# Keys and queries of the attention also stored in residue order, in blocks of 512 columns

## The chip, the cores and the metric

The kernel runs on one core of one Trainium2 chip. The metric is the device time of one execution in microseconds (us). Three runs before the change took 2612.30, 2614.26 and 2615.44 us; their median is 2614.26 us.

## What is computed

One step of a layer with two mixers, for a prompt of 2048 positions and 8 sample rows. The change touches mixer A, attention with 6 heads of 64, in three dilated branches:

```python
DILATED_BRANCHES = ((128, 1), (512, 4), (2048, 16))
def dilated_prompt(q, k, v, rel_bias, window, dil):
    nk = window // dil; blk = nk; unit = blk * dil
    ...
    qb = to_blocks(q)                 # (B, nb, blk, dil, H, E)
    kc = with_prev(to_blocks(k))
    vc = with_prev(to_blocks(v))
    ...
    s = jnp.einsum('bnqrhe,bnkrhe->bnrhqk', qb, kc) * scale + bias
    s = jnp.where(mask[None, :, None, None], s, NEG)
    lse = jax.nn.logsumexp(s, axis=-1)
    p = jnp.exp(s - lse[..., None])
    o = jnp.einsum('bnrhqk,bnkrhe->bnqrhe', p, vc)
out_a = rmsnorm(combine_branches([dilated_prompt(q, k, v, rel_bias, w, d) for (w, d) in DILATED_BRANCHES]))
```

A query at position t of a branch with dilation d meets the 128 keys before it at t-d, t-2d, ... and its own. In each branch 128 queries of one residue mod d therefore meet 128 keys of the same residue and, where there are any, the 128 before them. Mixer B (an mLSTM), the output projection and an MLP follow; the change leaves them alone.

## The kernel before

The program is written for a layer that orders each engine's instructions at build time; engines then run their lists in order. Stages, in the order of the program:

- `norm_and_v`: normalises the prompt, turns it into `XT` (two halves of the columns, each as a high and a low fp32r part) and projects v.
- `project_qk` (L913): for k, then q, and for each of three groups `j` of 128 rows of weights (two heads each), six column blocks `BLK` of 340 or 344 positions. A block is 24 matmuls (8 slices by 3 products, `mm3`, L162) into a PSUM tile `pmm` (4 buffers). ScalarE (ACT) copies the result to `qhi` (rounded to fp32r), VectorE (DVE) forms the rest `qlo`, and SyncE (SP) issues the stores of both to DRAM, `q_d` and `k_d`, at L966. For k, ACT first copies to `qb`, and `to_rows` turns `qb` with TensorE (PE) transposes into rows for the output of the key cache (`kt`, L928 to L932). The bias tables (`setup_bias`) and the gates of mixer B (`setup_gates`) are set up between the k groups.
- `xbob`: the projections of mixer B, in two halves. Attention of the 8 sample rows (`sample_attn`) runs beside the first half, the prompt's attention (`attention`, L1043) beside the second half.
- The rest of `attention` is interleaved with `mlstm` by a ratio of 0.72 steps of attention to one of mLSTM.
- Output projection and MLP, to the end.

In `attention`, `load_head` (L1046) fetches, once per head, the bias tile `nb`, the queries `Q2` (64 partitions of the high part, 64 of the low part) and the keys `KH` and `KL` (the high part twice, the low part twice), each [128, 2048] fp32. Per head come the branches b = 2 (dilation 16), 1 (dilation 4) and 0 (dilation 1); per branch four groups `g` of four tiles of 128 queries. `front` (L1062) makes the scores of two tiles: per tile two matmuls, with the tile's queries as weights and 256 columns of `KH`, then of `KL`, as the moving operand. At dilation d both operands are read with a step of d elements (L1070 to L1077). DVE adds the bias and takes the minimum (L1079), ACT takes the exponential (L1081), `turn` transposes on PE, and `weigh` multiplies by the rows of v in `V` (one DMA per group, L1128; 4 buffers). Results go out as `R4` (L1108). All loads and stores of this stage are issued by SP, in one order.

## Time and profile before

| | us |
|---|---|
| median of three runs | 2614.26 |
| the profiled execution | 2603.53 |
| its span, first to last instruction | 2601.8 |
| k projection, about 107 to 192 | 85 |
| q projection, about 192 to 262 | 70 |
| mixer B projections, first half, sample attention | 262 to 400 |
| attention of the prompt | 399.5 to 1000 |
| of it beside the second half of `xbob` | 400 to 532 |
| output projection and MLP | from about 1000 |

The matmul entries of a trace overlap: an entry's duration runs from its start to its modelled end, and the next starts before that. What a matmul takes from the engine is the distance between the starts of successive rows. In the lines of groups the columns are busy time, then the mean of one in ns, then the engine's idle time just before and what ended it.

### The profile page before, as it was taken

The page shows a single profiled execution, that of the slowest core. Times are in us where ns is not written, and L with a number is a line of the kernel's source. Part 1 is how long each engine was busy: PE and PEld are TensorE (multiplying, and loading weights), DVE is VectorE, ACT ScalarE, POOL GpSimd, SP SyncE. Part 2 cuts the span into 40 slices and gives each one's busy share as a digit, 9 for nine tenths or more (in the row PEclk, how much of TensorE's full clock was granted, in tenths as well). Part 3 has the DMA queues.
Part 4 walks back from the last instruction along what each step waited for, and adds up shares of the span by engine and source line. Part 5 has one row for each costly group of instructions (what it writes and reads, how often), then busy time and mean ns, then how long its engine had stood idle before and what let it go on. Part 6 is the DMA issues. An engine that isn't in the chain of part 4 may idle for free. (4 is left out here: it accounts for less than half of the span.)

```text
span 2601.8 us, 41795 instructions
## 1 busy us (share of the span) xinstructions
PE 2494.7 (96%) x15646; PEld 2252.6 (87%) x15646; DVE 1762.8 (68%) x3163; ACT 1157.7 (44%) x2205; POOL 861.8 (33%) x435
## 2 busy tenths in 40 slices
PE   8999999999999998899999999999999999999996
PEld 7989999997888886688788778887799999999996
DVE  6333755663876658665577996778967777676875
ACT  5431223333445544333466335653345643456333
POOL 1000000002432323211435785447753333543331
PEclk9999999997999999999999999999999999999998
DMA  7674656735768645875766768758687542765332
GB/s 199 156 195 149 177 152 169 185 100 147 189 171 190 170 132 147 261 232 155 244 224 227 274 231 285 238 203 291 212 268 244 189 129 94 244 217 165 109 118 75
DMA packets 470831, 491.64 MB, mean 189 GB/s; under 512 B 116376, under 2 KB 387124, under 8 KB 466917
## 3 DMA queue, kind: packets, MB, share of 16 engines
q1 hardware_dynamic: 468804, 485.36, 61.8%
q0 software_dynamic: 1536, 3.10, 0.5%
q8 instruction: 123, 2.02, 0.3%
q14 instruction: 80, 0.65, 0.1%
q10 hardware_dynamic: 288, 0.53, 0.1%
HBM read 380.49 MB, written 124.56 MB: 194 GB/s over the span
## 5 line engine op out<-in xcount | busy, mean ns | idle before, releaser
L74 DVE TENSOR_TENSOR al<-ax,ah 128x1024 fp32r<-128x1024 f32 x222 | 396.0, 1787 | 156.8 <-ACT ah L74 156.2
L74 POOL TENSOR_TENSOR ax<-ax,ay 128x1024 f32<-128x1024 f32 x117 | 313.2, 2677 | 310.8 <-DMA ay<-in_w_ff_dram 277.3
L1577 PE MATMUL pf<-bl,ah 128*128 128x258 f32 (+1 forms) x1344 | 360.7, 323 | 10.2 <-DVE bl L74 10.2
L1543 PE MATMUL pf<-bh,ah 128*128 128x258 f32 (+1 forms) x1344 | 359.8, 322 | 10.6 <-DVE R L74 9.5
L1543 PE MATMUL pf<-bh,al 128*128 128x258 f32 (+1 forms) x1344 | 357.6, 321 | 1.6 <-DVE al L74 1.6
L1577 PE MATMUL pf<-bh,al 128*128 128x258 f32 (+1 forms) x1344 | 358.6, 321 | 0.0
L1543 PE MATMUL pf<-bl,ah 128*128 128x258 f32 (+1 forms) x1344 | 358.1, 321 | 0.0
L1577 PE MATMUL pf<-bh,ah 128*128 128x258 f32 (+1 forms) x1344 | 351.6, 322 | 6.0 <-ACT bh L74 2.9
L74 ACT ACTIVATE ah<-ax 128x1024 fp32r<-128x1024 f32 x222 | 233.8, 1054 | 216.6 <-PE pf L1577 108.5
L74 POOL TENSOR_TENSOR bx<-R,R 128x1024 f32<-128x1024 f32 (+1 forms) x80 | 245.8, 3080 | 253.7 <-DVE bl L74 253.7
L74 DVE TENSOR_TENSOR bl<-bx,bh 128x1024 fp32r<-128x1024 f32 (+1 forms) x131 | 272.7, 2086 | 35.8 <-ACT bh L74 35.2
L1577 PEld LDWEIGHTS pf<-bl,ah 128*128 128x128 f32 x1344 | 225.1, 190 | 32.9 <-DVE bl L74 13.9
L1543 PEld LDWEIGHTS pf<-bh,ah 128*128 128x128 f32 x1344 | 224.2, 190 | 31.8 <-issue 8.7
L163 PE MATMUL pmm<-x,wh 128*128 128x344 f32 (+1 forms) x768 | 249.1, 324 | 0.0
L1577 PEld LDWEIGHTS pf<-bh,ah 128*128 128x128 f32 x1344 | 223.7, 190 | 29.2 <-DVE acc L74 4.3
L165 PE MATMUL pmm<-x,wl 128*128 128x344 f32 (+1 forms) x768 | 246.6, 321 | 0.0
L164 PE MATMUL pmm<-x,wh 128*128 128x344 f32 (+1 forms) x768 | 246.1, 321 | 0.0
L1543 PEld LDWEIGHTS pf<-bh,al 128*128 128x128 f32 x1344 | 224.0, 190 | 21.6 <-DVE al L74 1.8
L1543 PEld LDWEIGHTS pf<-bl,ah 128*128 128x128 f32 x1344 | 224.7, 190 | 19.5
L1577 PEld LDWEIGHTS pf<-bh,al 128*128 128x128 f32 x1344 | 224.3, 190 | 18.9
L74 ACT ACTIVATE R<-R 128x512 f32<-128x512 f32 (+1 forms) x256 | 161.1, 630 | 126.7 <-DVE R L74 122.6
L74 DVE TENSOR_TENSOR R<-R,pf 128x512 f32<-128x512 f32 (+1 forms) x256 | 165.2, 682 | 57.0 <-PE pf L1543 35.6
(471 smaller groups left out, 4813.7 us busy)
## 6 DMA issues: line engine op xcount, KB each, us to landing
ax<-in_w_ff_dram SPq DMA_DIRECT2D x184, 512.0 KB
ay<-in_w_ff_dram SPq DMA_DIRECT2D x120, 512.0 KB
sum_d<-ax SPq DMA_DIRECT2D x40, 512.0 KB
ax<-sum_d SPq DMA_DIRECT2D x40, 512.0 KB
xt<-in_x_prompt_dram SPq DMA_DIRECT2D x31, 512.0 KB
bx<-h_d SPq DMA_DIRECT2D x26, 516.0 KB
bx<-h_d SPq DMA_DIRECT2D x26, 512.0 KB
by<-h_d SPq DMA_DIRECT2D x22, 516.0 KB
```

The source lines that it names most:

```text
L74: return tc.keep_in_program_order(f(*a, **k))
L163: pe.matmul(out, lh, rh, start=first, stop=False)
L164: pe.matmul(out, lh, rl, start=False, stop=False)
L165: pe.matmul(out, ll, rh, start=False, stop=last)
L1543: pe.matmul(pf[:, n, :w], x_, y_[:, n * w:n * w + w], start=fst, stop=lst)
L1577: pe.matmul(pf[:, n, :w], x_[:, i, dsl], y_[:, n * w:n * w + w], start=a, stop=b)
```

## The change

1. DRAM holds k twice (`k_d[0]` in natural order, `k_d[1]` in blocks of 512 with 16 residues of 32 positions each) and q three times (natural; in blocks of 512 with 4 residues of 128; all 2048 as 16 residues of 128).
2. The projections of k and q run in blocks of 512 columns, the last as 256 and 264. After `qhi` and `qlo`, one ACT copy and one DVE copy put each block in residue order (`qhd`, `qld`), and for q a second pair of copies fills `q16`. The stores grow from two arrays for each of k and q to four for k and six for q. `kt` has one buffer instead of two, and its rows go out in one DMA per block.
3. `load_head` is split. `load_q` fetches the queries of one branch, `load_k` the keys in one of the two orders. They are issued at g == 1 of the branch before (`Q2`, `KH`, `KL` still have two buffers each). Per head that is three loads of queries and two of `KH` and `KL`, in place of one each.
4. `front` reads queries contiguously in all branches, and keys in runs of 32 elements in branches 1 and 2. In branch 1 the keys of a block then stand in another order, so `load_bias_of` permutes the bias with one ACT copy per head, and `load_v` fetches the rows of v with four DMAs per group.

```diff
-    q_d = [dram.tile([DA, S], F32, name=f"q{x}_d") for x in "hl"]
-    k_d = [dram.tile([DA, S], F32, name=f"k{x}_d") for x in "hl"]
+    q_d, k_d = ([[dram.tile([DA, S], F32, name=f"{y}{x}{v}_d") for x in "hl"] for v in range(n)]
+                for y, n in (("q", 3), ("k", 2)))
...
-    def proj(psp, tag, wh, wl, bi):
-        b0, n = BLK[bi]
-        b0 -= 1024 * (bi // 3)
-        xh, xl = XT[bi // 3]
+    def proj(psp, tag, wh, wl, b0, n):
+        xh, xl = XT[b0 // 1024]
+        b0 %= 1024
...
+        by = lambda t, d: t.rearrange("p (z r) -> p r z", r=d)
+        on = lambda t, d: t.rearrange("p (r z) -> p r z", r=d)
+        q16 = []
...
+                pt = pst.tile([P, 4, P], F32, name="ptp", tag="t")
+                for i in range(4):
+                    pe.transpose(pt[:, i], qb[:, i * P:i * P + P], ident)
+                kt = ev.tile([P, 4, P], F32, name="kt", bufs=1)
+                act.activation(kt, pt, AF.Copy)
                 ko = O["p_k"][0, 0].rearrange("t h e -> t (h e)")[:, j * P:(j + 1) * P]
-                nc.sync.dma_start(ko[b0:b0 + 2 * P].rearrange("(i p) c -> p i c", p=P), kt[:, :2])
-                nc.sync.dma_start(ko[b0 + 2 * P:b0 + m], kt[:w, 2])
-            if last:
+                nc.sync.dma_start(ko[512 * g:512 * g + 512].rearrange("(i p) c -> p i c", p=P), kt)
...
+                for g in (range(4) if which == "k" else (3, 0, 1, 2)):
+                    b0 = 512 * g
+                    hi = ev.tile([P, 512], F32R, name="qhi")
+                    lo = ev.tile([P, 512], F32R, name="qlo")
+                    qb = None
+                    if which == "k" or g == 3:
+                        qb = ev.tile([P, 520], F32, name="qb", bufs=3)
+                    for c0, n in ((0, 512),) if g < 3 else ((0, 256), (256, 264)):
+                        ps = proj(psm, "mm", wh, wl, b0 + c0, n)
+                        if later:
+                            to_rows(*later.pop())
+                        m = min(n, 512 - c0)
+                        cs = slice(c0, c0 + m)
+                        if which == "k":
+                            act.activation(qb[:, c0:c0 + n], ps[:, :n], AF.Copy)
+                            split(hi[:, cs], lo[:, cs], qb[:, cs])
+                        else:
+                            act.activation(hi[:, cs], ps[:, :m], AF.Copy, scale=-0.125)
+                            vec.scalar_tensor_tensor(lo[:, cs], ps[:, :m], -0.125, hi[:, cs].bitcast(F32),
+                                                     op0=OP.mult, op1=OP.subtract)
+                            if n > m:
+                                act.activation(qb[:, 512:], ps[:, m:n], AF.Copy, scale=-0.125)
+                    d = 16 if which == "k" else 4
+                    hd_ = ev.tile([P, 512], F32R, name="qhd")
+                    ld_ = ev.tile([P, 512], F32R, name="qld")
+                    act.activation(on(hd_, d), by(hi, d).bitcast(F32), AF.Copy)
+                    vec.tensor_copy(on(ld_, d), by(lo, d).bitcast(F32))
+                    for v, two in enumerate(((hi, lo), (hd_, ld_))):
+                        for dd, tt in zip(dst[v], two):
+                            nc.sync.dma_start(dd[j * P:(j + 1) * P, b0:b0 + 512], tt.bitcast(F32))
+                    if which == "q":
+                        if g == 3:
+                            q16 = [ev16.tile([P, 16, P], F32R, name=f"q16{x}") for x in "hl"]
+                        act.activation(q16[0][:, :, 32 * g:32 * g + 32], by(hi, 16).bitcast(F32), AF.Copy)
+                        vec.tensor_copy(q16[1][:, :, 32 * g:32 * g + 32], by(lo, 16).bitcast(F32))
+                        if g == 2:
+                            for dd, tt in zip(dst[2], q16):
+                                nc.sync.dma_start(dd[j * P:(j + 1) * P], tt.rearrange("p r z -> p (r z)").bitcast(F32))
+                    if qb is not None:
+                        later.append((which, j, g, qb))
...
+                    ev16 = pool(sset, "ev16", 1, "right")
+        sset.close()
...
+        def load_bias_of(h):
+            nb = wk.tile([P, 640], F32, name="nb")
+            raw = wk.tile([P, 256], F32, name="nbr", bufs=1)
+            load_bias(raw, 1, h)
+            for b in (2, 0):
+                o, w = NBW[b]
+                load_bias(nb[:, o:o + w], b, h)
+            act.activation(nb[:, 256:512].rearrange("p (k r z) -> p k r z", k=2, r=4),
+                           raw.rearrange("p (k z r) -> p k r z", k=2, r=4), AF.Copy)
+            return nb
+
+        def load_pairs(h, *sets):
             hs = slice(HD * h, HD * h + HD)
-            nb = wk.tile([P, 640], F32, name="nb")
-            for b, (o, w) in enumerate(NBW):
-                load_bias(nb[:, o:o + w], b, h)
-            Q, KH, KL = (wk.tile([P, S], F32, name=x) for x in ("Q2", "KH", "KL"))
-            for dst, lo, hi in ((Q, q_d[0], q_d[1]), (KH, k_d[0], k_d[0]), (KL, k_d[1], k_d[1])):
+            for dst, lo, hi in sets:
                 nc.sync.dma_start(dst[:HD], lo[hs])
                 nc.sync.dma_start(dst[HD:], hi[hs])
-            return nb, Q.bitcast(F32R), KH.bitcast(F32R), KL.bitcast(F32R)
+            return [t.bitcast(F32R) for t, _, _ in sets]
+
+        def load_q(h, b):
+            return load_pairs(h, (wk.tile([P, S], F32, name="Q2"), *q_d[b]))[0]
+
+        def load_k(h, v):
+            return load_pairs(h, *((wk.tile([P, S], F32, name=n), x, x) for n, x in zip(("KH", "KL"), k_d[v])))
...
+        def load_v(V, b, g, h):
+            if b == 1:
+                rs = HD + 1
+                for r in range(4):
+                    nc.sync.dma_start(V[32 * r:32 * r + 32],
+                                      bass.AP(tensor=v_d.tensor, offset=v_d.offset + (h * S + 512 * g + 4 * r) * rs,
+                                              ap=[[16 * rs, 32], [rs, 4], [1, rs]]))
+            else:
+                nc.sync.dma_start(V, rows(v_d, b, g, HD + 1, h * S * (HD + 1), HD + 1))
...
+            g4 = lambda t: t.rearrange("p (g r z) -> p g r z", r=16, z=32)
+            g44 = lambda t: t.rearrange("p (g k r z) -> p g k r z", k=4, r=4, z=32)
             ex = wk.tile([P, 2, 256], F32, name="ex", bufs=3)
             s_ = ps.tile([P, 2, 256], F32, name="ps_s", tag="s", bufs=2)
             for e, (a, w, mn, vts) in enumerate(tiles):
                 for i, K in enumerate((KH, KL)):
-                    if w == 256:
-                        mv, out, c0 = K[:, a - P * d:a + (P - 1) * d + 1:d], s_[:, e], 0
-                    elif b == 0:
-                        mv, out, c0 = K[:, 0:256], s_[:, e], 0
+                    out, c0 = s_[:, e], 0
+                    q = Q[:, a:a + P]
+                    if b == 0:
+                        mv = K[:, max(a - P, 0):max(a - P, 0) + 256]
+                    elif b == 1:
+                        g, t = a // 512, a % 512 // P
+                        if w == 256:
+                            mv = g44(K)[:, g - 1:g + 1, :, t]
+                            out = out.rearrange("p (k r z) -> p k r z", k=2, r=4)
+                        else:
+                            mv = g44(K)[:, g, :, t - e:t - e + 2].rearrange("p k r z -> p r k z")
+                            out, c0 = out.rearrange("p (k r z) -> p k r z", k=2, r=4), e * P
                     else:
-                        mv = K.rearrange("p (z x r) -> p z r x", x=P, r=d)[:, a // (P * d), (a - e) % d:(a - e) % d + 2]
-                        out, c0 = s_[:, e].rearrange("p (r x) -> p r x", r=2), e * P
-                    pe.matmul(out, Q[:, a:a + (P - 1) * d + 1:d], mv, start=i == 0, stop=i == 1)
+                        mv = g4(K)[:, :, a // P - e:a // P - e + 2].rearrange("p g r z -> p r g z")
+                        out, c0 = out.rearrange("p (r g z) -> p r g z", r=2, g=4), e * P
+                    pe.matmul(out, q, mv, start=i == 0, stop=i == 1)
...
-        hd = load_head(0)
+        nb, kk, qq = load_bias_of(0), {1: load_k(0, 1)}, load_q(0, 2)
...
-            cur = hd
             for b in (2, 1, 0):
                 vprev = None
-                if b == 0 and h + 1 < HA:
-                    hd = load_head(h + 1)
+                cur = nb, kk[min(b, 1)], qq
                 for g in range(4):
+                    if g == 1:
+                        if b:
+                            qq = load_q(h, b - 1)
+                        if b == 2:
+                            kk[0] = load_k(h, 0)
+                        elif b == 0 and h + 1 < HA:
+                            nb, kk[1], qq = load_bias_of(h + 1), load_k(h + 1, 1), load_q(h + 1, 2)
                     V = wk.tile([P, 4, HD + 1], F32, name="V", bufs=4)
-                    nc.sync.dma_start(V, rows(v_d, b, g, HD + 1, h * S * (HD + 1), HD + 1))
+                    load_v(V, b, g, h)
...
-                            a = (512 * g + P * t, 512 * g + t, 4 * g + t)[b]
+                            a = 512 * g + P * t
```

The order of the instructions moves at these places. SP, in the middle of the q projection: before, two stores a block, with the weights of mixer B (`wraw`) among them.

```order
L966 DMA ql_d<-qlo 128x340
L966 DMA qh_d<-qhi 128x344
L966 DMA ql_d<-qlo 128x344
L966 DMA qh_d<-qhi 128x344
L896 DMA wraw<-in_w_in_dram 128x8x128
L966 DMA ql_d<-qlo 128x344
```

The same place now, the last block of a group of q; `qhd`, `qld` are the block in residue order, `q16h`, `q16l` all 2048 columns in 16 residues.

```order
L969 DMA qh_d<-qhi 128x512
L969 DMA qh_d<-qhd 128x512
L969 DMA ql_d<-qlo 128x512
L969 DMA ql_d<-qld 128x512
L977 DMA qh_d<-q16h 128x2048
L977 DMA ql_d<-q16l 128x2048
```

Four stores now stand for each block, and two more, of 1 MB each, for every fourth block.

SP at the end of the q projection, before: loads of the sample attention (`qbr`, `kx`, `ky`) stand among the stores of the last group of q.

```order
L966 DMA ql_d<-qlo 128x344
L532 DMA qbr<-qs_d 128x384 x2
L966 DMA qh_d<-qhi 128x340
L966 DMA ql_d<-qlo 128x340
L532 DMA qbr<-qs_d 128x384 x2
L966 DMA qh_d<-qhi 128x340
L520 DMA kx<-in_cache_win_k_dram 128x384
```

Now, from the last stores of q on:

```order
L977 DMA qh_d<-q16h 128x2048
L977 DMA ql_d<-q16l 128x2048
L1015 DMA xbT_d<-xb 128x344
L1040 DMA cT_d<-c 128x344
L1048 DMA G_d<-g1t 128x344
L1049 DMA G_d<-so 128x344
L1015 DMA xbT_d<-xb 128x340
L512 DMA nb_2787<-tb_d 48x3x384
L1040 DMA cT_d<-c 128x340
L532 DMA qbr<-qs_d 128x384
```

The loads of the sample attention now come behind all stores of q and the first of `xbob`. Its transposes on PE stand where they stood among the projections.

SP at the start of the prompt's attention, before: one set of loads, then `V` for two groups.

```order
L1054 DMA KH<-kh_d 64x2048
L1053 DMA KL<-kl_d 64x2048
L1054 DMA KL<-kl_d 64x2048
L1128 DMA V<-v_d 128x260 x2
L1002 DMA xbT_d<-xb 128x344
```

Now: `Q_4128` is branch 2 of head 0, `Q_4158` and the `KH` and `KL` behind it are for its branches 1 and 0.

```order
L1073 DMA Q_4128<-qh_d 64x2048
L1074 DMA Q_4128<-ql_d 64x2048
L1096 DMA V<-v_d 128x260
L1073 DMA Q_4158<-qh_d 64x2048
L1074 DMA Q_4158<-ql_d 64x2048
L1073 DMA KH<-kh_d 64x2048
L1074 DMA KH<-kh_d 64x2048
L1073 DMA KL<-kl_d 64x2048
L1074 DMA KL<-kl_d 64x2048
L1096 DMA V<-v_d 128x260
```

Six loads of 512 KB stand ahead of the second `V`. On PE the score matmuls stand among the projections and the mLSTM's matmuls much as before, in the same number.

48 lines of the change are left out of this document (6 added, 42 removed).

## The prediction

> **What bounds the kernel now.** I read the stages first (busy time of the engines in stretches of the span), because the change touches only 107 to 262 us and 400 to 1000 us. The columns are the stretch, its length, then PE, PE's weight loads, DVE, ACT and POOL with their counts, the granted clock of PE, the DMA share and GB/s.
>
> ```profile
> core 0: us, PE busy (x) PEld busy (x) DVE busy (x) ACT busy (x) POOL busy (x), PEclk, DMA share, GB/s
> 107.00:192.00 85.00, 79.38 (x505) 76.41 (x504) 26.41 (x84) 29.54 (x81) 3.79 (x8) 0.98 0.71 195
> 192.00:262.00 70.00, 70.00 (x452) 69.74 (x451) 23.04 (x45) 13.51 (x28) 0.00 (x0) 1.00 0.52 154
> 262.00:400.00 138.00, 137.26 (x911) 136.45 (x910) 89.61 (x222) 36.31 (x70) 0.00 (x0) 1.00 0.61 170
> 400.00:532.00 132.00, 130.49 (x845) 127.24 (x845) 79.05 (x285) 51.17 (x114) 0.00 (x0) 1.00 0.67 167
> 532.00:700.00 168.00, 160.45 (x1024) 139.45 (x1023) 97.45 (x343) 68.16 (x191) 38.46 (x40) 0.92 0.53 136
> 700.00:900.00 200.00, 191.95 (x1349) 172.88 (x1348) 134.66 (x458) 100.24 (x309) 71.87 (x64) 0.98 0.75 185
> 900.00:1000.00 100.00, 95.46 (x687) 85.72 (x686) 62.01 (x225) 49.55 (x151) 22.60 (x22) 1.00 0.47 121
> ```
>
> PE is the bound in each: it is never idle in the q projection and idle 1.5 of 132 us from 400 on; from 532 to 1000 its idle time is 7.6 + 8.0 + 4.5 = 20 us of 468. DVE, the next, is busy in 294 us of those 468. Less work on PE should therefore shorten the stages. Where a trace shows PE's entries one after another, the distance between starts is the price. These are three pieces of the timeline of PE, in branch 1 (dilation 4), branch 2 (dilation 16) and branch 0 (dilation 1):
>
> ```profile
> 842.45 0.58 PE L1077 MATMUL ps_s<-KH,Q 128*128 128x256 f32 x1
> 842.85 0.42 PE L1077 MATMUL ps_s<-KL,Q 128*128 128x256 f32 x1
> 843.08 0.46 PE L460 MATMUL nu<-v,A 128*128 128x161 f32 x2
> ...
> 818.56 0.59 PE L1077 MATMUL ps_s<-KH,Q 128*128 128x256 f32 x1
> 818.97 0.40 PE L1077 MATMUL ps_s<-KL,Q 128*128 128x256 f32 x1
> 819.18 0.57 PE L1105 MATMUL po<-V,pT 128*128 128x65 f32 x4
> ...
> 881.66 0.39 PE L1077 MATMUL ps_s<-KH,Q 128*128 128x256 f32 x1
> 881.89 0.28 PE L1077 MATMUL ps_s<-KL,Q 128*128 128x256 f32 x1
> 882.01 1.00 PE L1105 MATMUL po<-V,pT 128*128 128x65 f32 x8
> ```
>
> A tile's two score matmuls take 0.63 us in branch 1, 0.62 in branch 2 and 0.35 in branch 0, for the same 256 columns. Only the step between the elements that they read differs. The same is seen in the busy time of line 1077 in six stretches, branches 2, 1, 0 of head 3 and of head 4 (32 matmuls each; the columns are the length, PE, its weight loads, clock, DMA share and GB/s):
>
> ```profile
> 709.30:742.10 32.80, 12.45 (x32) 8.40 (x32) 0.95 0.75 208
> 742.10:774.30 32.20, 12.78 (x32) 8.66 (x33) 1.00 0.66 156
> 774.30:805.50 31.20, 7.97 (x32) 4.94 (x32) 1.00 0.82 184
> 805.50:835.40 29.90, 12.83 (x32) 8.38 (x33) 1.00 0.84 210
> 835.40:864.80 29.40, 12.79 (x32) 8.47 (x33) 1.00 0.69 153
> 864.80:899.00 34.20, 9.01 (x32) 5.57 (x33) 0.95 0.70 178
> ```
>
> **Scores.** There are 6 heads of 16 tiles, so 96 tiles in each branch. By the starts, 96 x (0.63 - 0.35) + 96 x (0.62 - 0.35) = 53 us of PE. By the stretches, branch 2 has a mean of 12.64, branch 1 of 12.79, branch 0 of 8.49, so 6 x (4.15 + 4.30) = 51 us. I take -52, which says that pieces of 32 elements are read like a whole row. No row shows such pieces: the bounds are branch 0's price (-52) and today's price (0), and a piece holds 32 neighbours where today's patterns hold one, so I take the first.
>
> How the scores fall on the two stages, and what PE waits for most in the second:
>
> ```profile
> 400.00:532.00 132.00, 39.26 (x130) 29.41 (x129) 1.00 0.67 167
> 532.00:1000.00 468.00, 153.80 (x446) 101.59 (x446) 0.96 0.61 154
> ...
> PE ps_s L1077 <- DVE R L1079: 8.1, 10, 2.3
> ```
>
> 130 of the 576 score matmuls, worth 12 of the 52 us, run where PE is hardly idle, and should come through whole; 40 us lie in the second stage. There the scores wait 10 times for one of the two `ps_s` buffers, which DVE frees at L1079. Cheaper scores come to that wait sooner, so it is what is late next. The stretches above hint at the size: branch 0's 31.2 and 34.2 us are no shorter than branch 1's 32.2 and 29.4, though its scores are 4.3 us cheaper (its stretches hold other shares of the mLSTM and the loads of the next head, so this is no measure). Bounds: none of the 40 us lost, or all. I take +10.
>
> **Projections in blocks of 512.** The rows of PE in the q projection, and of the MLP for 512 columns:
>
> ```profile
> 229.70 0.32 PE L163 MATMUL pmm<-x,wh 128*128 128x344 f32 x1
> 229.86 0.32 PE L164 MATMUL pmm<-x,wh 128*128 128x344 f32 x1
> ...
> 1401.32 0.40 PE L1543 MATMUL pf<-bl,ah 128*128 128x512 f32 x1
> 1401.55 0.39 PE L1543 MATMUL pf<-bh,al 128*128 128x512 f32 x1
> ```
>
> 344 columns take 0.16 us, 512 take 0.23, and a group of weights has 2056 columns before and after: 0 us. A 512 block is 24 x 0.23 = 5.5 us of PE, and the four `pmm` buffers now cover up to 22 us instead of 15.
>
> **Added copies.** The nearest rows, from the lines of groups:
>
> ```profile
> L159 ACT ACTIVATE qhi<-qb 128x344 fp32r<-128x344 f32 x12 | 5.9, 490 | 0.1
> L250 DVE COPY nb<-ptp 48x384 f32<-48x384 f32 x3 | 1.7, 550 | 1.1 <-PE ptp L249 1.0
> ```
>
> Both are 1.43 ns a column, 0.73 us for 512. A block of q needs `qhi`, `qhd`, `q16h` on ACT (2.2 us) and the three others on DVE (2.2), under 5.5 us of PE. Read with a step of 4 or 16 elements the copies may cost up to double, as the scores do; ACT then has 0.73 + 2 x 1.46 = 3.7 us a block, still covered: 0 us. Only without that cover would 24 extra copies of q on ACT show, as 18 to 35 us.
>
> The Trainium skill ("Advanced Engine Details and Errata", section "Memory Cachelines") says that SBUF has lines of 16 bytes and that an access pattern which meets each line once is slower. By it the steps of 16 and 64 bytes cost alike, as the rows of branches 1 and 2 do, runs of 32 fp32 cost as a whole row does, and it speaks against the added copies, which meet each line once: by it 3.7 us a block instead of 2.2, and the same sum.
>
> **Added stores.** An array of 384 x 2048 fp32 is 3.15 MB: k stores two more (6.3 MB), q four more (12.6 MB). In the first table the DMA engines' time per MB is 0.71 x 85 us / (195 GB/s x 85 us) = 3.6 us in the k stage and 0.52 x 70 / 10.8 MB = 3.4 in the q stage. So k grows by 23 us, from 60 to 83 of 85; q by 43, from 36 to 79 of 70, from which about 15 us leave, because the sample attention's loads (8 x 528 KB) move behind. That is nearly full. The sizes of these loads, and a store of the k stage that landed late:
>
> ```profile
> kx<-in_cache_win_k_dram SPq DMA_DIRECT2D x8, 192.0 KB
> qbr<-qs_d SPq DMA_DIRECT2D x8, 192.0 KB
> ky<-in_cache_win_k_dram SPq DMA_DIRECT2D x8, 144.0 KB
> ...
> DVE qlo L160 <- DMA kl_d<-qlo: 17.5, 2, 16.3
> ```
>
> The longer of the two waits was 16.3 us, and PE was idle only 85 - 79.4 = 5.6 us in all of that stage, so the `pmm` buffers covered most of it. `kt` with one buffer and the bursts of `q16` add to it. Bounds: 0, or the 7 us by which 83 + 79 exceed 155, plus one uncovered stall of 17. I take +3. The late sample loads cost 0: their last reduction on DVE started at 270.8 us, for a transpose at 316.1, so 20 us later is still in time.
>
> ```profile
> L540 DVE TENSOR_REDUCE sc<-ky x8: 542/544/548, 250.2 to 270.8; 97x6 f32<-97x384 f32 x8
> L559 PE MATMUL pt<-ident,sc x1: 273/273/273, 316.1 to 316.1; 128*48 128x128 f32 x1
> ```
>
> **Added loads.** Per head 7 MB instead of 3. The burst at the start of attention shows the price, six loads of 0.52 MB:
>
> ```profile
> 384.00:400.00 16.00, 16.00 (x103) 16.00 (x102) 9.68 (x27) 2.70 (x6) 0.00 (x0) 1.00 1.03 271
> ...
> SPq L1128 <- PE po L1105: 47.6, 19, 7.7
> ```
>
> At 271 GB/s, 3.15 MB take 11.6 us. A second such burst per head is now issued at g == 1 of branch 2, ahead of that group's `V`, and SP, which waited 19 times for a `V` buffer, will also wait for a `Q2` buffer, with `V`, results and the mLSTM's loads queued behind. Bounds: 0, or 6 x 11.6 = 70 us if PE waited out each burst. SP runs ahead of PE by the four `V` buffers, about one branch-stretch of 30 us, so most is covered; I take +4, nearest to a single exposed third of a burst in the first head, where `xbob` still shares the queue. The bias permutation is 6 ACT copies: 0.
>
> **Sum.** -52 + 10 + 0 + 0 + 3 + 4 = -35 us. The profiled execution took 2603.5 us (span 2601.8 and 1.7 around it), 10.7 under the median of the runs; on the median's scale 2614.3 - 35 = **2579 us**.
>
> **Rivals.**
> - *The stores become the bound.* The k and q stages run at the DMA's pace, `qhi` and `kt` wait, and PE loses the upper bound, 24 us, 21 more than I take: 2600. For it: 83 of 85 us. Against: the deeper cover in time of `pmm`. Chance 0.14.
> - *The change doesn't do what it says.* Pieces of 32 behind steps are read no faster, so PE's 52 us stay, and only the added work shows: 2614 to 2621. Against: a piece is 32 neighbours. Chance 0.09.
> - *Slower: loads in front of `V`.* PE waits for each head's second burst whole: -52 + 70 + 3 = +21, 2635 (the waits for DVE lie inside). It decides from where a burst delays `V` by over 49/6 = 8 us beyond SP's lead. For it: a DMA share of 0.75 already from 700 to 900. Against: the lead. Chance 0.09.
> - *The clock falls.* From 532 to 700 the granted clock was 0.92, in a stage where PE is idle 7.6 us. If more waiting brought all of 532 to 1000 there from its mean of 0.96, 4% of some 430 us, 17 us, would go back: 2596. Chance 0.06. The Trainium skill ("TensorE: Matmul & The Clock Gate", Part 1) has the clock halved after an idle window of PE; by it, it needs gaps of over 3 us, and the longest wait quoted here is 2.3.
>
> **How the numbers follow.** Forecast 0.62, its own range 2555 to 2597 (all of the 52 and a little more, or half of it). Range for 8 in 10: 2552 to 2616, which takes in the stores and the clock and leaves out the slower rival and part of "no effect". A measurement can tell 0.2%, 5 us, from no change. Faster: 0.62 + 0.14 + 0.06 = 0.82; the no-effect rival falls half in "same" and half in "slower", with 0.02 of the forecast's tail: same 0.06, slower 0.12.
>
> **What would show it.** Starts of a tile's score pair 0.35 us apart in all branches (scores right); the busy time of the score line near 8.5 us in each stretch; PE still without idle time from 192 to 262 and the same length of stage (stores and copies hidden); the stage from 400 to 1000 shorter by some 38 us; more waits of scores for DVE's L1079. I would be wrong if PE waited for `V`, if DVE or ACT waited for stores for longer than four blocks, or if the score pair stayed at 0.6.

## The result, and the profile after

The changed kernel takes 2695.23 us (median of 4 runs, 2689.69 to 2702.20) against 2614.85 us of the kernel before (2612.30 to 2616.28): a ratio of 1.0299, 95% interval 1.0277 to 1.0321. It is slower by 80 us; the prediction had 35 us faster.

The first view to read is again the one by stages, of the changed kernel, with the columns of the prediction's first table:

```profile
core 0: us, PE busy (x) PEld busy (x) DVE busy (x) ACT busy (x) POOL busy (x), PEclk, DMA share, GB/s
107.00:192.00 85.00, 80.66 (x468) 68.23 (x467) 34.27 (x97) 42.23 (x68) 3.85 (x8) 1.00 0.82 257
192.00:262.00 70.00, 70.00 (x370) 60.09 (x369) 28.95 (x53) 37.63 (x47) 0.00 (x0) 1.00 0.84 289
262.00:400.00 138.00, 130.31 (x822) 128.59 (x821) 88.47 (x217) 35.20 (x65) 0.00 (x0) 0.94 0.65 181
400.00:532.00 132.00, 117.07 (x776) 109.24 (x775) 74.49 (x268) 45.55 (x105) 0.00 (x0) 0.93 0.85 199
532.00:700.00 168.00, 148.42 (x915) 128.26 (x913) 85.04 (x302) 56.51 (x153) 22.73 (x28) 0.83 0.56 135
700.00:900.00 200.00, 163.89 (x1055) 138.28 (x1054) 108.84 (x367) 78.94 (x236) 62.38 (x54) 0.84 0.79 195
```

Nothing is lost up to 262 us: PE has no idle time in the q projection, with the stores at 289 GB/s, and the q projection even begins 3.8 us earlier (184.4 us, before 188.2). From 262 on two columns change together: PE is idle (36 of 200 us from 700 to 900, where it was 8), and its granted clock falls to 0.83.

The scores did become cheap. A piece of the timeline of PE in branch 1 of the changed kernel:

```profile
558.70 0.28 PE L1122 MATMUL ps_s<-KH,Q 128*128 128x256 f32 x1
558.81 0.28 PE L1122 MATMUL ps_s<-KL,Q 128*128 128x256 f32 x1
558.93 0.32 PE L163 MATMUL pmm<-x,wh 128*128 128x344 f32 x1
```

This pair takes 0.23 us, where the prediction's pair of branch 1 took 0.63. It is one of the cheapest: over the pairs of the two traces that run at full clock, with their rows and the next one side by side, the median is 0.32 us in branch 2 and 0.33 in branches 1 and 0, where it was 0.59, 0.63 and 0.33. So 96 x 0.27 + 96 x 0.31 = 55 us less.

To see what took that gain away I cut one stretch from the first score matmul to the last. This is its row in the kernel before, and behind it the one of the changed kernel (columns as above):

```profile
399.70:991.10 591.40, 569.84 (x3823) 517.55 (x3823) 366.22 (x1283) 266.53 (x756) 131.81 (x123) 0.97 0.63 158
```

```profile
416.40:1076.90 660.50, 576.28 (x3780) 500.45 (x3779) 353.92 (x1269) 267.00 (x757) 131.39 (x123) 0.87 0.74 177
```

Three numbers come out of such a row. Length minus PE's busy time is **idle** time: 21.6 before, 84.2 now. Length times (1 - clock) is what the clock took: 0.03 x 591.4 = 18, now 0.13 x 660.5 = 86. Part of that is time in which PE stood idle anyway and is counted already: by the trace's records of the clock, 16 of the 86 us and none of the 18. What PE **lost to the clock** while it worked is, by the same records, 17 before and 69 now. What is left is PE's **work** at full clock: 553 before, 507 now. So the stretch grew by 69 us although PE's work in it fell by 46: 63 us more idle, 52 us more lost to the clock. Some 6 of the 46 are not saved but moved: 41 of the matmuls of `xbob` (0.16 us each) now stand ahead of the first score. The other 20 us of the difference of spans (2691.1 - 2601.8 = 89.3) are 16.7 by which the scores begin later and 3.4 behind their end.

What PE and DVE waited for from 262 to 1085 us, changed kernel (total, times, longest; the last row is a wait at 304 us, ahead of the scores):

```profile
DVE sm L1124 <- DMA R_d<-R: 36.1, 5, 12.1
PE po L1150 <- DMA V<-v_d: 32.8, 5, 11.0
PE ps_s L1122 <- DVE R L1124: 22.3, 31, 3.2
...
PE pmm L163 <- ACT wh L159: 6.7, 1, 6.7
```

PE waited for `V`, up to 11 us at a time, at five places, each the second group of a branch, right behind a burst of `Q` and `K`. The first row shows a second thing behind the bursts: DVE could not write into an `R4` buffer until an earlier result's store had landed, and PE's scores waited for DVE.

### The profile page after: what moved, and what is told of

The parts are those of the page before. It is cut to its first block, busy times and chain, and to the rows that moved or that the text cites. A ratio compares the mean times of both kernels' runs of the same rounds, so it can differ in the third digit from the quotient of the medians.

```text
span 2691.1 us, 41645 instructions
## 1 busy us (share of the span) xinstructions
PE 2515.7 (93%) x15496; PEld 2230.1 (83%) x15496; DVE 1770.3 (66%) x3193; ACT 1197.3 (44%) x2214; POOL 873.1 (32%) x435
## 5 line engine op out<-in xcount | busy, mean ns | idle before, releaser
L74 POOL TENSOR_TENSOR ax<-ax,ay 128x1024 f32<-128x1024 f32 x117 | 322.4, 2756 | 297.5 <-DMA ay<-in_w_ff_dram 265.1
L74 DVE TENSOR_TENSOR bl<-bx,bh 128x1024 fp32r<-128x1024 f32 (+1 forms) x131 | 265.5, 2031 | 34.3 <-ACT bh L74 33.8
L163 PE MATMUL pmm<-x,wh 128*128 128x344 f32 (+4 forms) x720 | 243.8, 339 | 6.7 <-ACT wh L159 6.7
L1593 PEld LDWEIGHTS pf<-bh,al 128*128 128x128 f32 x1344 | 224.8, 190 | 21.6 <-DVE al L74 1.8
L165 PE MATMUL pmm<-x,wl 128*128 128x344 f32 (+4 forms) x720 | 241.8, 336 | 0.6 <-DVE wl L160 0.6
L164 PE MATMUL pmm<-x,wh 128*128 128x344 f32 (+4 forms) x720 | 240.6, 334 | 0.0
```

The costliest lines, as they stand in the source:

```text
L74: return tc.keep_in_program_order(f(*a, **k))
L163: pe.matmul(out, lh, rh, start=first, stop=False)
L164: pe.matmul(out, lh, rl, start=False, stop=False)
L165: pe.matmul(out, ll, rh, start=False, stop=last)
L1593: pe.matmul(pf[:, n, :w], x_, y_[:, n * w:n * w + w], start=fst, stop=lst)
```

## The experiments

Times are medians; ratios are to the kernel before in the same session. Idle, clock and work (us) are worked out as above, in the stretch from the first to the last score of each run; the clock column is the loss while PE worked, from the trace's records of the clock, since the row's two digits give it to 3 us only. In the kernel before, in e13 and in e16, 604 of `xbob`'s matmuls lie in this stretch, in e4 595, in e18 583, in all others 563.

| kernel | us | ratio (95%) | idle | clock | work | DMA share |
|---|---|---|---|---|---|---|
| before | 2614.85 | 1 | 22 | 17 | 553 | 0.63 |
| changed | 2695.23 | 1.0299 (1.0277 to 1.0321) | 84 | 69 | 507 | 0.74 |
| e1 K, Q loaded once | 2597.3 | 0.9934 (0.9909 to 0.9959) | 41 | 28 | 495 | 0.66 |
| e9 half the loads | 2635.95 | 1.0086 (1.0053 to 1.0118) | 47 | 45 | 503 | 0.73 |
| e2 V first | 2684.96 | 1.0269 (1.0239 to 1.0299) | 89 | 59 | 506 | 0.74 |
| e3 spread | 2698.69 | 1.0331 (1.0293 to 1.0369) | 85 | 76 | 513 | 0.72 |
| e4 POOL's queue | 2724.26 | 1.0425 (1.0385 to 1.0465) | 115 | 56 | 500 | 0.71 |
| e5 e2, more buffers | 2691.02 | 1.0297 (1.0249 to 1.0345) | 76 | 61 | 508 | 0.74 |
| e6 e2, R4 stored by ACT | 2732.69 | 1.0446 (1.0398 to 1.0494) | 117 | 87 | 502 | 0.68 |
| e7 e3, e5, e6 together | 2674.12 | 1.0229 (1.0181 to 1.0277) | 64 | 71 | 507 | 0.74 |
| e16 before, plus loads | 2638.01 | 1.0113 (1.0086 to 1.0140) | 33 | 31 | 551 | 0.73 |
| e18 half rows | 2695.69 | 1.0299 (1.0260 to 1.0338) | 90 | 60 | 510 | 0.72 |
| e10 weights by POOL | 2694.36 | 1.0306 (1.0271 to 1.0342) | 89 | 58 | 508 | 0.75 |
| e14 sample pool moved | 2695.94 | 1.0294 (1.0267 to 1.0320) | 86 | 52 | 510 | 0.76 |
| e13 forced waits | 2624.07 | 1.0029 (1.0013 to 1.0044) | 28 | 20 | 558 | 0.62 |
| e8 reorder, ACT | 2635.56 | 1.0081 (1.0054 to 1.0107) | 57 | 46 | 499 | 0.63 |
| e11 reorder, DVE | 2630.13 | 1.0047 (1.0023 to 1.0070) | 58 | 33 | 502 | 0.64 |
| e12 reorder, POOL | 2651.88 | 1.0137 (1.0103 to 1.0170) | 71 | 50 | 497 | 0.62 |
| e17 reorder, three engines | 2638.97 | 1.0128 (1.0090 to 1.0165) | 64 | 40 | 500 | 0.63 |
| e15 K on chip, Q with step | 2628.18 | 1.0044 (1.0026 to 1.0061) | 40 | 29 | 529 | 0.62 |

### Is it the added loads?

**e1** takes them away and leaves every other instruction; branches 1 and 0 then make their scores from keys and queries in the order of branch 2:

```diff
-                cur = nb, kk[min(b, 1)], qq
+                cur = nb, kk[1], qq
...
-                    if g == 1:
-                        if b:
-                            qq = load_q(h, b - 1)
-                        if b == 2:
-                            kk[0] = load_k(h, 0)
-                        elif b == 0 and h + 1 < HA:
-                            nb, kk[1], qq = load_bias_of(h + 1), load_k(h + 1, 1), load_q(h + 1, 2)
+                    if g == 1 and b == 0 and h + 1 < HA:
+                        nb, kk[1], qq = load_bias_of(h + 1), load_k(h + 1, 1), load_q(h + 1, 2)
```

> K and Q of a head are loaded once, in the order of branch 2, and serve all three branches (the scores of branches 1 and 0 are taken from keys and queries in the wrong order; the same number of instructions, 4 MB less of loads per head). Theory 1, the added loads are what costs (PE waits for V and others behind them, and the clock that falls with the waiting): the 52 us of the scores show, less some 10 for DVE, and some 17 stay lost ahead of the attention: about 2590 us (2570 to 2605), no wait of PE for V over 3 us, granted clock over 0.9 from 532 to 900. Rival A, the rest of the change costs it (V of branch 1 in four DMAs, biases, the waits for DVE): 2670 to 2700 as the changed kernel, waits for V stay.

Measured: 2597.3 us, 98 us under the changed kernel, and 14 under the kernel before in the same session (2611.56). Rival A, that the rest of the change is what costs, falls. The row of the stretch, and the wait of the scores for DVE:

```profile
421.80:986.20 564.40, 523.68 (x3782) 468.96 (x3781) 356.99 (x1273) 264.28 (x757) 130.91 (x123) 0.95 0.66 162
```

```profile
PE ps_s L1122 <- DVE R L1124: 17.1, 15, 3.4
```

The idle time is halved, the clock back at 0.95, and no wait for `V` is left among the largest. The rest of the change isn't free either: against the kernel before, e1 has 57 us less work in the stretch, but 19 us more idle and 11 more lost to the clock. PE's work is 495, where the changed kernel has 507; these 12 us have no explanation here.

**e9** leaves K's second load out and keeps Q's three:

```diff
-                cur = nb, kk[min(b, 1)], qq
+                cur = nb, kk[1], qq
...
-                        if b == 2:
-                            kk[0] = load_k(h, 0)
-                        elif b == 0 and h + 1 < HA:
+                        if b == 0 and h + 1 < HA:
```

> K is loaded once a head, in the order of branch 2 (branch 0 takes its scores from keys in the wrong order), Q three times: 5 MB a head, half of the added 4 MB. e1 (none of them) took 2597, the changed kernel (all) 2695. If each added MB costs the same, because PE waits in proportion and its clock falls with the waiting: 2635 to 2655. If the 2 MB fit into the engines' idle time and only the rest is too much: 2595 to 2610, and PE's idle time in the stage of the scores as in e1 (41 us) instead of 84.

```profile
419.60:1014.90 595.30, 547.86 (x3780) 482.38 (x3780) 351.36 (x1272) 267.56 (x757) 129.77 (x123) 0.92 0.73 175
```

Measured 2636: 39 us for the first 12 MB (over six heads; Q's loads), 59 for the other 12 (K's second load). Neither half is free. That the price rises with the amount isn't shown: by the intervals each of the two differences is good to some 10 us, and the halves are not the same kind of burst.

**e16** adds the loads to the kernel before, into a buffer that nothing reads:

```diff
+                    if (b, g) in ((2, 1), (2, 2), (1, 1)):
+                        hs = slice(HD * h, HD * h + HD)
+                        for src in {(2, 1): k_d + k_d, (2, 2): q_d, (1, 1): q_d}[b, g]:
+                            x = wk.tile([P, S // 2], F32, name="X", bufs=3)
+                            nc.sync.dma_start(x, src[hs].rearrange("h (t c) -> (h t) c", t=2))
```

> The kernel before, with 4 MB more of loads a head into a buffer that nothing reads (half of it 2 MB at g == 1 of branch 2, then 1 MB at g == 2 and 1 MB at g == 1 of branch 1); scores and order as before. If the added bytes cost what they cost in the changed kernel, whatever PE has to do: 2615 + 98 = 2713. If PE's longer scores (some 62 us more work in the stage by the traces) cover part of the loads, so that the gain of the reads and the cost of the loads can't both be read off alone: 2640 to 2680. If the loads are no cost by themselves: up to 2625.

```profile
400.30:1015.70 615.40, 582.15 (x3820) 526.59 (x3821) 357.90 (x1277) 268.05 (x755) 129.84 (x121) 0.94 0.73 190
```

Measured +29 us (2638.0 to 2609.0 in that session), between the ranges, just under the one for "cover". Two readings are possible and not separated: PE's longer work covers part of the loads, or these loads are cheaper. Their packets of 4096 bytes, over all 128 partitions, took a DMA engine 200 ns on average, those of `Q` and `K` (8192 bytes, 64 partitions) 578: per byte, 0.69 of the time.

**e18** was to tell whether the packet's length does that: each load of 64 rows split into two by columns.

```diff
-                nc.sync.dma_start(dst[:HD], lo[hs])
-                nc.sync.dma_start(dst[HD:], hi[hs])
+                for c in (slice(0, S // 2), slice(S // 2, S)):
+                    nc.sync.dma_start(dst[:HD, c], lo[hs, c])
+                    nc.sync.dma_start(dst[HD:, c], hi[hs, c])
```

> The changed kernel, with each load of Q and K (64 rows of 8192 bytes) split into two of 4096-byte rows; the same bytes, order and places. In the changed kernel a packet of 8192 bytes took a DMA engine 578 ns, in e16 one of 4096 bytes 200 ns, so the 40.3 MB of the stage would keep the engines busy 123 us instead of 178, and all of the stage 432 instead of 487. If the DMA engines' time is what the added loads cost (e1 374 us busy: 2597; e9 432: 2636; changed 487: 2695): 2630 to 2655. If it is the bytes, or the number of loads on SP's queue: 2685 to 2705.

Measured 2695.7, no change, but the premise failed: the 4096-byte packets took 265 ns, not 200, and the DMA engines' busy time went from 0.74 x 660.5 = 489 to 0.72 x 659.7 = 475 us, not to 432. So the length isn't it (64 partitions instead of 128 may be; not tried), and whether engine time or bytes set the price stays open.

### Which wait is it?

**e2** issues `V` ahead of the burst of loads:

```diff
+                    V = wk.tile([P, 4, HD + 1], F32, name="V", bufs=4)
+                    load_v(V, b, g, h)
                     if g == 1:
...
-                    V = wk.tile([P, 4, HD + 1], F32, name="V", bufs=4)
-                    load_v(V, b, g, h)
```

> At g == 1 the group's V is issued ahead of the burst of Q and K instead of behind it; the bytes are the same. Theory 1a, the order on the SP queue is what costs: the five waits of PE for V (32.8 us) and the clock they bring go: 2620 to 2650 us. Theory 1b, what is behind the burst counts whatever it is (the next group's V, the mLSTM's loads): the waits move by one group or to other tiles and the time stays at 2670 to 2700 us.

PE's waits for `V` (32.8 us in the changed kernel) are gone from the list. PE's waits for DVE have taken their place (22.3 before this edit), and the time (2685) can't be told from the changed kernel's by the intervals:

```profile
PEld ps_s L1122 <- DVE R L1124: 80.7, 62, 10.7
...
PE ps_s L1122 <- DVE R L1124: 65.4, 35, 10.6
...
DVE sm L1124 <- DMA R_d<-R: 37.5, 5, 11.0
```

The results' stores still stand behind the burst, and with three `R4` buffers DVE waits for them to land about as long as before (36.1 us in the changed kernel). **e5** is e2 with more buffers:

```diff
-                    V = wk.tile([P, 4, HD + 1], F32, name="V", bufs=4)
+                    V = wk.tile([P, 4, HD + 1], F32, name="V", bufs=6)
-                    R4 = wk.tile([P, 4, HD + 2], F32, name="R4", bufs=3)
+                    R4 = wk.tile([P, 4, HD + 2], F32, name="R4", bufs=6)
```

> As e2 (V ahead of the burst), with six buffers for R4 and for V instead of three and four. In e2 DVE waited 37.5 us for the store of R to land before it could write into an R4 buffer, and the scores waited 146 us (PE and its weight loads) for DVE. Theory 2, the results' stores stand behind the burst in the same queue and R4's three buffers run out: DVE's wait for R_d falls under 5 us and the time to 2620 to 2660 us. Rival B, the DMA engines have too much to move in this stage (e2: 110 MB from 400 to 1000 us): the waits move to Mb, the mLSTM's loads or SP, and the time stays within 1% of e2's 2685.

DVE's wait for the stores is gone from the list, and the time stays (2691). Of e5's waits:

```profile
PE ps_s L1122 <- DVE R L1124: 31.7, 46, 6.2
...
PE ppq L368 <- DMA cp<-cT_d: 19.8, 4, 13.0
```

Next in line is a load of the mLSTM (`cp`), up to 13 us. **e3** cuts the bursts into pieces of 1 MB, one a group, behind `V` (`load_k1` loads one of KH and KL):

```diff
+                    if b and g == 1:
+                        qq = load_q(h, b - 1)
+                    if b == 2 and g > 1:
+                        kk[0] = load_k1(h, 0, g - 2)
+                    if b == 0 and g and h + 1 < HA:
+                        if g < 3:
+                            kk[1] = load_k1(h + 1, 1, g - 1)
+                        else:
+                            nb, qq = load_bias_of(h + 1), load_q(h + 1, 2)
```

> The same bytes, V first, and Q and K in pieces of at most 1 MB, one per group of tiles, instead of 3, 1 and 3 MB at g == 1. Theory 1 (bursts): 1 MB is 4 us of the DMA engines against some 8 us of a group, so PE's waits for V vanish: 2590 to 2620 us. Rival B, the bytes themselves are too many for the stage (the DMA engines were busy 0.8 of it): the waits are spread, not gone, 2650 to 2690 us.

No gain (2699). **e4** moves the loads of Q and K to another queue, **e6**, which has e2's edit too, the results' stores:

```diff
e4: -                nc.sync.dma_start(dst[:HD], lo[hs])
e4: +                nc.gpsimd.dma_start(dst[:HD], lo[hs])
... (the same for dst[HD:])
e6: -                nc.sync.dma_start(dst, R4)
e6: +                nc.scalar.dma_start(dst, R4)
```

> The bursts as in the changed kernel, but issued by POOL on its own queue, so that V, the results and the mLSTM's loads no longer stand behind them in one queue; they share the DMA engines with them. Theory 1 (one queue in order): V waits at most for its share of the engines, 2600 to 2640 us. Rival B (bytes): 2670 to 2700 us, DMA share about 1.0 around the bursts and PE still waiting for V.

> As e2, but the stores of R4 are issued by ACT, which has just made R4, on its own queue: SP no longer waits for ACT (56 + 35 us in e2) and the loads behind those stores are issued earlier. Theory 3, SP standing at the R4 stores is what leaves the DMA engines idle between bursts: 2610 to 2650 us. Rival B (bytes): no change from e2's 2685, or slower, since a small store shares the engines with the burst (as in e4, where DVE waited 105 us for R).

Both are slower than the changed kernel, by 29 and 37 us. One row of each, e4 first, shows a common part: DVE waits for the results' stores 18 and 22 times, where it was 5. That these stores land late because they share the DMA engines with a burst fits, but isn't shown.

```profile
DVE sm L1124 <- DMA R_d<-R: 104.8, 18, 13.4
```

```profile
DVE sm L1124 <- DMA R_d<-R: 83.7, 22, 12.4
```

In e4 the larger part lies elsewhere. Its scores begin at 441.5 us instead of 416.4, and ahead of them PE stood idle once for 23.1 us, until 435.1; the stretch of the scores is 671 us against 661.

**e7** is the edits of e3, e5 and e6 in one kernel:

> e3, e5 and e6 together: V first, Q and K in pieces of 1 MB, six buffers of R4 and V, stores of R4 by ACT; the same bytes. If what is lost is order and buffers, this gets nearly all of it back: 2590 to 2615 us. If it is the amount (rival B: the DMA engines' work in the stage grew from 371 us in 591 to 487 us in 661, and the forecast had it in 553), 2640 us or more.

2674: 21 of the 98 us come back, with an interval that just touches the changed kernel's. So no single wait holds the loss. Take one away and the next load or store that is late takes its place.

### What lowers the clock?

In all these rows the us lost to the clock are 0.5 to 1.1 times the us idle. **e13** was to force waits without any load: in the kernel before, 18 times, PE turns a block, ACT and POOL copy it, and PE reads the copy.

```diff
+            turns[0] += 1
+            if turns[0] % 8 == 5:
...
+                pe.transpose(pt[:, 0, 0], ident, ident)
+                act.activation(t1, pt[:, 0, 0], AF.Copy)
+                gp.memset(t3, 0.0)
+                gp.tensor_copy(t2[:, :P], t1)
+                gp.tensor_copy(t2[:, P:], t3[:, P:])
+                gp.tensor_copy(t3, t2)
+                pe.transpose(pt[:, 0, 0], t3[:, :P], ident)
```

> The kernel before, with 18 waits of PE made by hand, one in each branch of each head: PE turns a block, ACT copies it, POOL copies it three times, and only then PE goes on (nothing else is changed). The trace says how long PE then idles; I expect some 2 to 3 us each, 35 to 55 us more than the 22 of before. If idle time of PE halves its clock behind it, as the traces of e1 to e12 suggest (us lost to the clock about as many as us idle), 30 to 50 us more are lost to the clock, which was 17 before, and the time is 2680 to 2715. If the low clock has another cause (the DMA traffic), the clock's loss stays below 25 us and the time is at most 2670.

The waits didn't come about: the layer that orders the instructions put other work of PE between the two transposes, the idle time grew by 6.5 us only, and the time by 0.3%. The test says nothing about the cause. What speaks against the traffic as the cause are e8, e11, e12 and e17 (below): DMA share 0.62 to 0.64, as before the change, idle 57 to 71 us, and 33 to 50 lost to the clock, where the kernel before lost 17. That the idle time causes the loss is likely from the pattern, not shown by an intervention; and it isn't all of it, for in e13 6.8 us were lost to the clock between 256 and 405 us, where PE was idle for 0.7 us in all.

### Why do the scores begin 17 us late?

**e10** loads `xbob`'s first weights on POOL's queue, **e14** puts the sample attention's pool on the other side of SBUF:

```diff
e10: -            xw = load_w(base, rem)
e10: +            xw = load_w(base, rem, nc.sync if sb else nc.gpsimd)
... (the same for ow)
e14: -        sp = pool(sA, "spa", 2, "right")
e14: +        sp = pool(sA, "spa", 2, "left")
```

> The changed kernel, with the weights of xbob's first half loaded on POOL's queue, past the sample attention's loads, which now stand ahead of them on SP's. In the changed kernel PE waited 6.7 us for wh at 304 us, the clock was halved for 6.8, 6.8 and 3.4 us behind it, and the scores began 17 us later than before (416.4 to 399.7). If that wait is the cause, the scores begin at 400 to 406 and the time is 2680 to 2688; if the larger pool of the projection (the sample loads start late whatever the queue) is, the start stays at 412 to 417 and the time at 2695.

> The changed kernel, with the pool of the sample attention on the other side of SBUF, so that its loads need not wait until the projection's larger pools (evq, ev16) are free. If that wait is what makes PE idle at 304 us and the scores begin 17 us late: they begin at 400 to 406, PE's idle time and clock loss from 262 to the scores fall from 16 to under 4 us, and the time is 2678 to 2686. If not: start at 412 to 420 and 2695.

Neither helps: the scores begin at 420.7 and 421.3 us, the times are 2694.4 and 2695.9. In e8 and e15, which store as much as the kernel before, they begin at 414.9 and 417.8, so the added stores aren't it either. In e13, which changes nothing ahead of the scores, they begin at 405.3, so some 6 us lie between runs.

What the 17 us are made of can be read from the traces. These are the stretches from the first matmul of `xbob` to the first score, before and changed:

```profile
256.50:399.70 143.20, 142.46 (x945) 141.65 (x943) 94.17 (x230) 39.19 (x73) 0.00 (x0) 1.00 0.62 173
```

```profile
252.80:416.40 163.60, 155.91 (x984) 154.16 (x983) 104.79 (x257) 45.13 (x80) 0.00 (x0) 0.95 0.70 196
```

`xbob` begins 3.7 us earlier. Then come 7.0 us more of idle time, 7.1 lost to the clock while PE worked, and 6.3 of work: 877 of `xbob`'s matmuls, not 836, stand ahead of the first score, in e10, e14, e8 and e15 as well. So 6 of the 17 us are work that the scores' stretch no longer has. Of the idle time 6.7 us are one wait for `wh`, which ACT makes from weights (`wraw`) that had just landed. In e10 PE waits 7.4 us for `wl`, the other part of these weights, in e14 7.5 for `wh`, so neither edit removed the wait; why the weights come late stays open.

### Can the gain be kept without the loads?

**e8** stores and loads K and Q once, in the order of branch 2 (bytes as before), and makes the other orders in SBUF, one copy of 128x512 in each step of branches 2 and 1. **e11** and **e12** have the copies on DVE and POOL, **e17** has KH on ACT, KL on DVE and Q on POOL.

```diff
...
+            kk[0] = [new("KH"), new("KL")]
+            for src, dst in zip(kk[1], kk[0]):
+                for g in range(4):
+                    act_copy(blk(dst, g).rearrange("p (z r) -> p z r", r=16),
+                          blk(src.bitcast(F32), g).rearrange("p (r z) -> p z r", r=16))
+                    yield
...
e11: -            act.activation(o, i, AF.Copy)
e11: +            vec.tensor_copy(o, i)
e12: -            act.activation(o, i, AF.Copy)
e12: +            gp.tensor_copy(o, i)
```

> K and Q are stored and loaded once, in the order of branch 2 (as many bytes as the kernel before), and ACT makes the orders of branches 1 and 0 in SBUF: 16 copies of 128x512 a head, one per step of branches 2 and 1, 96 in all, about 0.73 us each by the copies of qhi = 70 us of ACT, which was busy half of this stage. If the added bytes are the cost and contiguous reading the gain, this is e1's 2597 less up to 10 us for the stores that go, plus what the copies hold up of ACT's exp: 2585 to 2610 us. If ACT's copies stand in the path from DVE's min to the transposes, 70 us come back: 2650.

> e8 with the 96 copies on DVE. ACT took 1.11 us for one (107 us in all; a copy of 512 without a step takes it 0.60), DVE 0.62 in the projection (qld), so 60 us of DVE, which was busy 350 of e1's 564 us. If e8's 38 us over e1 came from ACT's long copies standing ahead of its exp, this is 2600 to 2620; if any copy on an engine of that path costs about its length, 2640 to 2660, since DVE is the busier one.

> e8 with the 96 copies on POOL, which was busy 161 of 660 us up to the end of the scores and is not on the path from the scores to the transposes. Its operations on 512 columns took 1.3 us, so some 125 us of POOL. If the path is what counts: e1's time and a little, 2595 to 2615. If POOL's copies delay Mb, G2c and the mLSTM with them, or slow DVE beside them: 2620 to 2650.

> e8 with its 96 copies shared out: KH on ACT, KL on DVE, Q (both orders) on POOL, so 27 us of ACT, 16 of DVE and 54 of POOL. If e8, e11 and e12 lost 33 to 55 us against e1 because one engine had all copies: 2600 to 2618, level with the kernel before. If every copy delays the engine's next step, wherever it stands: 2625 to 2645.

2636, 2630, 2652 and 2639: PE's work is nearly as small as in e1 (497 to 502 against 495), but each way 33 to 55 us come back, nearly all as idle time and clock, on any engine, shared out or not. The price of a copy is not what I had assumed for ACT. This is the changed kernel in the q and k stages (groups by line; busy time, mean ns):

```profile
L965 ACT ACTIVATE qhd<-qhi 128x512 fp32r<-128x512 f32 x24 | 27.1, 1127 | 1.2 <-DMA kh_d<-qhd 0.5
L966 DVE CAST qld<-qlo 128x512 fp32r<-128x512 f32 x24 | 15.0, 626 | 0.6
...
L159 ACT ACTIVATE qhi<-qb 128x512 fp32r<-128x512 f32 x9 | 5.7, 632 | 0.2
```

ACT needs 1.13 us with a step and 0.63 without, both from SBUF to SBUF; DVE 0.63 with one.

**e15** reorders K alone, in half as many copies (KH on ACT, KL on DVE) and reads Q from its natural order with a step, as weights, as the kernel before did (the sample pool as in e14):

```diff
-                    q = Q[:, a:a + P]
+                    n, d = a // P, BRANCHES[b][1]
+                    a0 = (a, n // 4 * 512 + n % 4, n)[b]
+                    q = Q[:, a0:a0 + (P - 1) * d + 1:d]
```

> A version meant to keep the gain: K stored and loaded once in the order of branch 2, its natural order made on chip (KH by ACT, KL by DVE, 48 copies instead of 96), Q loaded once in natural order and read with a step by the weight loads, as before the change; the sample pool as in e14. e11 (96 copies on DVE) took 2630. If the step in Q costs nothing on PE (its weight loads took 0.30 instead of 0.19 us but run beside the matmuls) and half the copies cost half: 2575 to 2605, the first below the kernel before. If weight loads of 0.30 hold the matmuls up (2 x 0.12 us of matmul a tile): PE's work goes back towards before and the time is 2610 to 2635.

```profile
417.80:1015.00 597.20, 557.69 (x3783) 506.88 (x3782) 374.36 (x1298) 285.63 (x778) 130.55 (x123) 0.95 0.62 154
```

2628. The idle time is smaller with fewer copies (40), though PE's longer work may also cover part of it, and PE's work is 529, 34 more than e1's 495: the second case of the expectation. So of the some 51 us that contiguous reads gain in e1 (57 less 6 moved), about 34 lie in the weight loads of Q, the rest in K.

None of the versions beats the kernel before; the only one faster is e1, which leaves loads out and computes other scores.

## Why the prediction was wrong, step by step

- **Scores, -52.** Right. The pairs of matmuls take the same 0.32 to 0.33 us in all branches, which makes 55 us; by PE's work the gain is 51 us in e1 and some 40 in the changed kernel (57 and 46, less 6 moved). Pieces of 32 are read like a row; the rival "doesn't do what it says" falls.
- **Scores waiting for DVE, +10.** This wait itself is about right where no added loads disturb: 17.1 us in e1 against 8.5 before, in the same stretch. But it was not all that cheaper scores bring: in e1 the idle time rose by 19 us, and 11 more were lost to the clock.
- **Blocks of 512, copies, stores: 0, 0, +3.** Nothing was lost in their own stages: `xbob` begins 3.7 us earlier than before. ACT's 1.13 us for a copy with a step is under the bound of 1.46, and it was covered. As the prediction says of it, the Trainium skill ("Advanced Engine Details and Errata", section "Memory Cachelines") has such reads slower; ACT's two rows (1.13 and 0.63 us) agree, and DVE has no row of such a copy without a step to compare.
- **Late sample loads, 0.** The scores begin 17 us late, which no term had. I checked the one consumer (the transpose at 316.1) and not what is issued behind these loads: PE waited 6.7 us for `wh` at 304 us, and in that stretch its clock fell as well (0.94 from 262 to 400). Moving either thing that I suspected (e10, e14) did not bring it back, so that the sample loads are the cause is not shown. Some 6 of the 17 us are moved work. That the scores stand among the projections much as before, as I wrote of the change, missed this.
- **Added loads, +4.** This is the step that failed: they cost 98 us (e1). The sentence "SP runs ahead of PE by the four `V` buffers, about one branch-stretch of 30 us, so most is covered" took `V` for the only thing behind the bursts, and the lead for a fixed stock. The lead was smaller to begin with: in the kernel before, SP issued a group's `V` between 6 and 43 us before PE came to it, in the median 24. The bursts then used it up. SP's wait for a free `V` buffer, which shows that it has its full lead, was 47.6 us in the prediction's row and is this in the changed kernel:

```profile
SPq L1096 <- PE po L1150: 7.7, 5, 3.8
```

  At the two longest waits `V` was issued 3.2 us before and 1.0 us after PE came to it, and PE then stood for 11 us. The first of them, on SP and on PE:

```profile
508.43 0.59 SPq L1096 DMA_DIRECT2D V<-v_d  x1
...
522.60 0.66 PE L1150 MATMUL po<-V,pT 128*128 128x65 f32 x2 [10.93 <-DMA V<-v_d]
```

  And `V` is not the only thing behind the bursts: with `V` ahead (e2) the time stayed, DVE waiting for the results' stores (37.5 us) and, with more buffers (e5), PE for `cp` (19.8). The balance that I made for the stores' stages (added MB by us per MB against the stage's length) I did not make here: 0.63 x 591 = 373 us of DMA before, 24 MB more give 489 as measured, in a stage that I had at 553: 0.88 of it, with several small transfers that PE needs within a few us.
- **The rival "loads in front of V", +21, 0.09.** The right direction, half of the mechanism, and too small an upper bound: I took "PE waits out each burst" (70 us) as the most that could happen. The idle time alone was 63 us more, but only 33 of it were waits for `V`; what went beyond was the clock.
- **The rival "the clock falls", 17 us, 0.06.** 52 us in the scores' stretch and 7 ahead of it. I had dismissed it with a rule of the Trainium skill ("TensorE: Matmul & The Clock Gate", Part 1), that the clock is halved after an idle window of some 3.4 us. The trace of the kernel before already spoke against that; here PE stood 2.47 us, until 737.5 us (columns: stretch, length, PE busy, clock, DMA share, GB/s):

```profile
737.00:739.00 2.00, 1.49 (x9) 0.87 1.04 256
739.00:741.00 2.00, 2.00 (x10) 0.50 0.31 98
741.00:743.00 2.00, 2.00 (x16) 0.78 0.00 0
743.00:745.00 2.00, 2.00 (x15) 1.00 0.31 72
```

  The clock was halved behind it for 3.4 us. The measurement decides: here a shorter wait than the rule's went ahead of a halving.

In sum: -46 of work, +63 idle, +52 clock in the scores' stretch, +17 ahead of it and +3 behind it: +89, as the two spans differ.

## What to carry to other kernels

Before adding traffic to a stage, add up the DMA engines' busy time there against the length that you hope for, not the present one: at 0.79 of it (e9, 435 of 553 us) this kernel lost 39 us, at 0.88 it lost 98, and no order, queue or number of buffers that was tried gave more than 21 of them back: in e2 and e5 the next small transfer took the place of the one that was helped. Work that is taken from the busiest engine takes away the cover of everything beside it (e1's idle time rose by 19 us with no load added), so price the next waits at the shortened stage. And count each us that PE stands idle as more than one here: over these runs 0.5 to 1.1 us lost to the clock went with it.

## What the runs showed of the hardware

- PE's clock was granted at a half in pieces of 3.4 us and multiples of it (one of 44 us in the changed kernel, from 602 us), also behind waits of 1.3 to 2.5 us (five times in the kernel before) and at two places with no wait of over 0.5 us in the 12 us before (changed, 1042.5 us; e9, 796.1 us).
- A load of 64 rows into 64 partitions took 578 ns for a packet of 8192 bytes and 265 for one of 4096, 14 and 15 GB/s for an engine; one of 128 rows of 4096 bytes into 128 partitions took 200 ns, 20 GB/s. The two differ in the source's layout too.
- A copy of 512 columns with a step in its input took 1.13 us on ACT (0.63 without), 0.63 to 0.78 on DVE, and in e12, on POOL:

```profile
L1084 POOL CAST Q<-Q 128x512 fp32r<-128x512 f32 x48 | 53.7, 1158 | 59.9 <-PE pt L1158 38.8 <-PE ps_s L1145 21.0
```
